# A squared-ReLU MLP by rows with a seven-product block scheme, and a small tile of its own for attention's lowest scores

## The chip, the core and the metric

The kernel runs on one core of one Trainium2 chip. The core has five engines that run side by side, each through its own instructions in order: TensorE (PE, matrix products into PSUM; PEld is its loading of the stationary operand), VectorE (DVE), ScalarE (ACT), GpSimd (POOL) and SyncE (SP, which here issues most of the DMAs). They wait for each other by semaphores. The metric is the device time of one execution in microseconds (us).

## The reference

One layer of a bidirectional encoder on 2048 tokens of 1024 features, all in float32:

```
y = rmsnorm(h) @ w_in                    # q, k, v and two convolution inputs
h = h + [dilated attention || conformer convolution] @ w_out
h = h + cross_attention(rmsnorm(h), rmsnorm(mem))
u = rmsnorm(h) @ w_up                    # 1024 -> 4096
h = h + square(relu(u)) @ w_down         # 4096 -> 1024
out = rmsnorm(h)                         # final gain norm_final_g
```

The attention has three patterns (window and dilation 128/1, 512/4, 2048/16) for each of eight heads; their outputs are weighted by a softmax over the three log-denominators. The change touches the last two lines for a quarter of the tokens, and one step of the second attention pattern.

## The kernel before

**Products in float32.** `mm3` (L198 to L201) makes each float32 product of three matmuls: each operand is split into a part that TensorE's float32r form holds and a remainder (`h` and `l`), and high x high, high x low and low x high are summed in PSUM. A weight tile is loaded by DMA (`raw`), its high part is made by a cast on ACT (L190, `whi`) and its remainder by a subtraction on DVE (L191, `wlo`); `wpost` does the three steps. Pairs of `whi` and `wlo` lie in two pools (`wp`, `wq`) with two buffers each, and `turn_w` deals them out by turns, so four pairs go round. There are two buffers for `raw`.

**Tokens.** They go in four groups of 512 (`p` = 0 to 3). `post(p)` does for one group the output projection, cross attention, the MLP and the final norm. While `post(p)` runs, the attention and the convolution of group p+1 are woven in; the last group, p = 3, has nothing woven in.

**MLP before.** Activations lie with features on the partitions and tokens along the row: the residual `hs[m]` is eight tiles of 128 features x 512 tokens. The 4096 hidden features go in eight feature groups (`fg`). Each makes four up products of 128 hidden features (24 matmuls of 128 x 128 by 128 x 512 each); DVE takes the ReLU times the row scale (L1321, `rl`), ACT squares it (L1322) and makes the high part (L1323), DVE the remainder (L1324). Then `down` makes eight products, with the weights stationary and the hidden tokens moving, 12 matmuls each, and DVE adds each PSUM result to `hs[m]` (L1339). So a feature group is 96 + 96 matmuls. In the last feature group, `add_sq` sums the squares for the final norm.

**The end before.** In the last token group the last feature group's down product is done in two halves of 256 tokens, and `final` follows each half: the root of the mean square (`rstd_from`: a matmul with ones, then DVE, a power on POOL at L177, and three small DVE operations), the gain (L1360), transposes to rows on TensorE (L1367, four to a PSUM bank), scaling by the root (L1369 on ACT, L1371 on DVE), and the DMA to the output.

**Second pattern of the attention.** `unit` works on two blocks of queries of one head. `att_probs` (L773) adds the mask to the scores and writes the lowest (scores carry the opposite sign) beside the outputs, into column HD+1 of a tile `os_` (`o1` for the second pattern), from which the DMA to `oscr` stores the pair of heads. The group p = 0 (`far`) does the third pattern with it.

**Order.** The lists of instructions are not in the code's order. The framework traces the program and a planner (`schedule_with_timeline_sim=True`) places each engine's instructions; `weave` and `pinned` only bound it. A tile's buffer is used again when its last readers are done.

Of the kernel before, what the change touches and what calls it, by code (L numbers as in the profile page):

```python
# [10 lines left out]
F32 = mybir.dt.float32  # L11
# [36 lines left out]
def hybrid_layer(ctx, tc, A, out):  # L48
# [148 lines left out]

    def mm3(o, lh, ll, rh, rl, first, end):  # L198
        PE.matmul(o, lh, rh, start=first, stop=False)  # L199
        PE.matmul(o, lh, rl, start=False, stop=False)  # L200
        last["pe"] = PE.matmul(o, ll, rh, start=False, stop=end)  # L201

# [752 lines left out]
    def att_units(p, far, then):  # L955
# [4 lines left out]
        vt = {}  # L960
        o1 = [None]
        order = (1, 0) if far else (0, 1)
# [256 lines left out]
    def post(p):  # L1219
# [87 lines left out]
        FG = 8  # L1307
        end = p == NG - 1
        for fg in range(FG):
# [16 lines left out]
            if fg == FG - 1:  # L1326
                fsum = ssum_tile(f"f{p}")
                if not end:
                    load_cat(p + 1, 0)

            def down(mp2, t, w, wh, wl):
                sl = slice(t, t + w)
                for e in range(2):
                    m = 2 * mp2 + e
                    es = slice(P * e, P * e + P)
                    pt = ps("mm", "dn")[:, 0:w]
                    for k in range(4):
                        mm3(pt, wh[:, k, es], wl[:, k, es], hh["h", k][:, sl], hh["l", k][:, sl], k == 0, k == 3)
                    last["dve"] = DVE.tensor_tensor(hs[m][:, sl], hs[m][:, sl], pt, op=ALU.add)  # L1339
                    if fg == FG - 1:  # L1340
                        add_sq(hs[m][:, sl], fsum[:, sl], m == 0)

            wd = []
            for mp2 in range(4):
                wd.append(wpost(wcols(w_down, mp2 * 256, 256, (4 * fg, 4 * fg + 4)), f"d{p}{fg}_{mp2}", (P, 4, 256)))
                if fg == FG - 1 and end:
                    continue
                down(mp2, 0, 512, *wd[-1])
                yield


        fin = {}

        def final(t, w):
            r = rstd_from(fsum[:, t:t + w])
            sl = slice(t, t + w)
            for k in range(KC):
                if t == 0:
                    fin[k] = ytile("h", k, f"fin{p}_{k}", F32)
                DVE.tensor_scalar(fin[k][:, sl], hs[k][:, sl], gain("final", k), None, op0=ALU.mult)  # L1360
            for j in range(w // P):
                c0 = t + P * j
                for g in range(2):
                    ot = ytile("l", 2 * (c0 // P) + g, f"ot{p}{c0}{g}", F32)
                    pt = ps("T", "ot")
                    for i in range(4):
                        PE.transpose(pt[:, P * i:P * i + P], fin[4 * g + i][:, c0:c0 + P], ident)  # L1367
                    if g:
                        ACT.activation(ot, pt, AF.Copy, scale=r[:, j:j + 1])  # L1369
                    else:  # L1370
                        DVE.tensor_scalar(ot, pt, r[:, j:j + 1], None, op0=ALU.mult)  # L1371
                    dma(out[0, 512 * p + c0:512 * p + c0 + P, 512 * g:512 * (g + 1)], ot)
                yield

        if end:
            for t in range(0, 512, 256):
                for mp2 in range(4):
                    down(mp2, t, 256, *wd[mp2])
                yield from final(t, 256)
        else:  # L1380
            load_cat(p + 1, 1)
            yield from final(0, 512)

# [74 lines left out]
```

## Time and profile before

| what | us |
|---|---|
| median of 3 runs (lowest to highest) | 2891.43 (2891.17 to 2894.11) |
| the profiled execution, its own time | 2888.26 |
| its span, first to last instruction | 2886.5 |
| granted TensorE clock, mean | 0.994 of full speed |
| first up matmul of the last group's MLP | at 2520.93 |
| first matmul of its last down product | at 2850.69 |
| its last matmul of a down product | at 2876.05 |

A row of a timeline reads: start, duration, engine, line, operation, written tile, read tiles, shape, count, and in brackets how long the engine had been idle before and what ended that. The recorded duration of a matmul, 0.39 us, contains its way through the array, which overlaps the next one's; the time that a matmul costs is read from start to start. A row of groups has the line, the shape and the count, then the busy time and the mean duration in ns, then the idle time before and its releasers. The windows give each engine's busy time and its instructions in a stretch of the span.

### The profile page before, as it was taken

What the parts mean: (1) busy time and instruction counts of PE and PEld (TensorE: products, weight loads), DVE (VectorE), ACT (ScalarE), POOL (GpSimd) and SP (SyncE); (2) the same over time, 40 slices, a digit from 0 to 9 for tenths busy, and PEclk for the clock granted to TensorE, in tenths of its full rate; (3) what the DMA queues carried; (4) which work ended last, traced back from release to release, by engine and by line L of the source; (5) the groups of instructions that cost most, each with busy time, mean ns of one, the idle gap of its engine ahead of it and who ended that gap; (6) DMA issues with size and microseconds to landing.
All of it is one profiled execution on the core that took longest, in us unless ns stands there. A gap on an engine that the chain in (4) does not pass through costs nothing.

```text
span 2886.5 us, 41313 instructions
## 1 busy us (share of the span) xinstructions
PE 2826.6 (98%) x15628; PEld 2376.2 (82%) x15628; DVE 1857.6 (64%) x3306; ACT 1166.3 (40%) x1988; POOL 458.0 (16%) x469
## 2 busy tenths in 40 slices
PE   8999999998999999999999999999999999999999
PEld 7878899887788888888888888888888888888887
DVE  5636535565789776557887765689876555544445
ACT  5633211475554333434543343444333433432233
POOL 1336421122102011200012012002011200000000
PEclk9999999999999999999999999999999999999999
DMA  8979845799734444554444446534543445333332
GB/s 264 295 173 228 202 132 131 182 256 247 205 102 131 135 133 123 168 160 145 121 130 130 138 117 192 175 96 128 142 127 109 139 132 175 93 90 101 96 95 74
DMA packets 598632, 433.74 MB, mean 150 GB/s; under 512 B 191550, under 2 KB 524786, under 8 KB 597921
## 3 DMA queue, kind: packets, MB, share of 16 engines
q1 hardware_dynamic: 558256, 408.21, 50.2%
q10 hardware_dynamic: 37952, 16.88, 2.4%
q0 software_dynamic: 2224, 6.01, 0.6%
q8 instruction: 123, 2.02, 0.3%
q14 instruction: 77, 0.62, 0.1%
HBM read 339.89 MB, written 91.11 MB: 149 GB/s over the span
## 4 chain that ended last, share of the span: by engine, by line
PE 82%; DVE 9%; DMA 5%; issue 2%; ACT 2%; POOL 1%; SPq 1%; POOLq 0%; DVEq 0%; ACTq 0%
PE dn L199 8%; PE dn L200 8%; PE dn L201 8%; PE up L199 7%; PE up L200 7%; PE up L201 7%; PE lin L199 4%; PE lin L201 4%; PE lin L200 4%; DVE cacc L216 3%; PE o L199 2%; PE o L200 2%; PE o L201 2%; PE xs L199 2%; PE xs L201 2%; PE xs L200 2%
## 5 line engine op out<-in xcount | busy, mean ns | idle before, releaser
L199 PE MATMUL dn<-hhh,whi_d 128*128 128x512 f32 (+1 forms) x1056 | 402.8, 392 | 7.2 <-DVE h L1339 6.1
L200 PE MATMUL dn<-hhl,whi_d 128*128 128x512 f32 (+1 forms) x1056 | 403.4, 385 | 1.1 <-DVE hhl L1324 1.1
L199 PE MATMUL up<-mh,whi_u 128*128 128x512 f32 x1024 | 402.9, 393 | 0.5 <-DVE rl L1321 0.5
L201 PE MATMUL dn<-hhh,wlo_d 128*128 128x512 f32 (+1 forms) x1056 | 402.6, 384 | 0.0
L200 PE MATMUL up<-ml,whi_u 128*128 128x512 f32 x1024 | 399.4, 390 | 1.0 <-DVE ml L1214 0.9
L201 PE MATMUL up<-mh,wlo_u 128*128 128x512 f32 x1024 | 399.7, 391 | 0.0
L216 DVE SCALAR_TENSOR_TENSOR cacc<-cu,cw,cacc 128x512 f32<-128x512 f32 x480 | 389.0, 811 | 5.5
L190 ACT CAST whi_d<-raw_d 128x1024 fp32r<-128x1024 f32 x128 | 134.6, 1052 | 418.1 <-PE up L200 378.6
L1339 DVE TENSOR_TENSOR h<-h,dn 128x512 f32<-128x512 f32 (+1 forms) x264 | 172.3, 667 | 162.9 <-PE dn L201 161.7
L190 ACT CAST whi_u<-raw_u 128x1024 fp32r<-128x1024 f32 x128 | 134.4, 1050 | 327.2 <-PE dn L200 304.1
L1321 DVE SCALAR_TENSOR_TENSOR rl<-up,ssumx 128x512 f32<-128x512 f32 x128 | 88.0, 690 | 256.9 <-PE up L201 252.6
L199 PEld LDWEIGHTS dn<-hhh,whi_d 128*128 128x128 f32 x1056 | 198.1, 189 | 47.5 <-DVE h L1339 10.2
L201 PEld LDWEIGHTS dn<-hhh,wlo_d 128*128 128x128 f32 x1056 | 198.8, 188 | 39.7
L200 PEld LDWEIGHTS dn<-hhl,whi_d 128*128 128x128 f32 x1056 | 199.3, 189 | 37.4 <-DVE hhl L1324 2.0
L200 PEld LDWEIGHTS up<-ml,whi_u 128*128 128x128 f32 x1024 | 192.4, 188 | 40.1 <-DVE ml L1214 2.3
L201 PEld LDWEIGHTS up<-mh,wlo_u 128*128 128x128 f32 x1024 | 192.2, 188 | 40.3
L199 PEld LDWEIGHTS up<-mh,whi_u 128*128 128x128 f32 x1024 | 192.4, 188 | 38.5 <-DVE rl L1321 0.9
L774 ACT ACTIVATE sm<-sm,o 128x256 f32<-128x256 f32 (+1 forms) x384 | 160.1, 466 | 126.3 <-DVE o L773 125.9
L773 DVE CUSTOM_DVE_ANT_0 sm<-s,mask 128x256 f32<-128x256 f32 (+1 forms) x384 | 128.5, 375 | 83.5 <-PE s L999 39.4
L191 DVE TENSOR_TENSOR wlo_u<-raw_u,whi_u 128x1024 fp32r<-128x1024 f32 x128 | 158.4, 1237 | 32.7 <-ACT whi_u L190 32.4
L191 DVE TENSOR_TENSOR wlo_d<-raw_d,whi_d 128x1024 fp32r<-128x1024 f32 x128 | 163.2, 1275 | 23.8 <-ACT whi_d L190 23.7
L177 POOL TENSOR_TENSOR nr<-st_v,mhalf 128x4 f32<-128x4 f32 (+1 forms) x13 | 13.0, 997 | 839.2 <-DVE st_v L173 839.2
(403 smaller groups left out, 6320.9 us busy)
## 6 DMA issues: line engine op xcount, KB each, us to landing
raw_u<-in_w_up_dram SPq DMA_DIRECT2D x128, 512.0 KB
raw_d<-in_w_down_dram SPq DMA_DIRECT2D x128, 512.0 KB
raw_o<-in_w_out_dram SPq DMA_DIRECT2D x32, 512.0 KB
raw_a<-ascr SPq DMA_DIRECT2D x32, 512.0 KB
raw_b<-bscr SPq DMA_DIRECT2D x32, 512.0 KB
k<-kscr SPq DMA_DIRECT2D x24, 512.0 KB
k<-kscr SPq DMA_DIRECT2D x8, 1152.0 KB
xn<-in_x_dram SPq DMA_DIRECT2D x32, 256.0 KB
```

The source lines that it names most:

```text
L177: POOL.tensor_tensor(dst, v, mhalf.to_broadcast([P, v.shape[1]]), op=ALU.pow)
L190: ACT.copy(hi, raw)
L191: (lo_eng or DVE).tensor_tensor(lo, raw, f(hi), op=ALU.subtract)
L199: PE.matmul(o, lh, rh, start=first, stop=False)
L200: PE.matmul(o, lh, rl, start=False, stop=False)
L201: last["pe"] = PE.matmul(o, ll, rh, start=False, stop=end)
L216: DVE.scalar_tensor_tensor(acc, u[:, t:t + 512], cw[:, c, t:t + 1], acc, op0=ALU.mult, op1=ALU.add)
L773: last["dve"] = DVE.tensor_tensor_reduce(dst, so, mask[:, 256 * m:256 * m + nk], 1.0, 3e38, ALU.add, ALU.min, mn)
L774: last["act"] = ACT.activation(dst, dst, AF.Exp, bias=mn, scale=-1.0)
L1321: last["dve"] = DVE.scalar_tensor_tensor(r, pt, 0.0, rsb, op0=ALU.max, op1=ALU.mult)
L1339: last["dve"] = DVE.tensor_tensor(hs[m][:, sl], hs[m][:, sl], pt, op=ALU.add)
```

## The change

1. *The last token group's MLP becomes `last_mlp`.* In feature group 0 the residual is transposed to rows, 128 tokens x 1024 features in four row tiles (`to_rows`, eight sets of four transposes, between up matmuls). The up products stay. The down product is now made by rows: the hidden tokens are stationary (128 at a time) and the weights move, 512 columns at a time.
2. *Seven block products for eight*, in feature groups 0 to 6. The hidden part is cut in 2 x 2 blocks of 256 tokens x 256 hidden features, the weights in 2 x 2 blocks of 256 x 512. Winograd's form of Strassen's scheme has seven block products of sums and differences of these blocks. `parts` makes the four sums of the hidden blocks on DVE and splits seven blocks in high and remainder (ACT and DVE); `sums` and one line in `seven` make four sums of weight blocks on DVE, in place in tiles that the attention had used (`room`); `piece` splits each of the seven. A product's PSUM bank is added to the row tiles by DVE, also where the next product goes on summing in the same bank (`skip_group_check`): 14 additions per feature group in place of 8.
3. *The last feature group* has plain products by rows, one row tile after the other; squares are summed along the row by ACT, and each row tile is scaled by root and gain on DVE and stored. No transposes follow, and no half products.
4. *The lowest scores of the second pattern*, in groups 1 to 3, go to a tile `low1` with two buffers, and POOL copies them beside the outputs before the store.
5. The padding tile at the head of the pool `top` shrinks from 296 to 256 columns, by what the new small tiles take, so that the tiles behind keep their addresses.

Up products, the splitting, the first seven stages and the code of groups 0 to 2 are otherwise the same; the code of `down` and `final` for them only loses its halves.

```diff
-    top.tile([P, 296], F32, name="tpad")
+    top.tile([P, 256], F32, name="tpad")
...
+                if not far:
+                    low1[0] = top.tile([P, 4, 2], F32, tag="low1", name=f"low1_{p}{pr}", bufs=2)
             os_ = o1[0] if pat else o0
+            lows = low1[0] if pat and not far else os_[:, :, :, HD + 1]
...
-                              os_[:, blk, hh, HD + 1:HD + 2]))
+                              lows[:, blk, hh:hh + 1]))
...
             if g and hh and pat:
+                if not far:
+                    POOL.tensor_copy(os_[:, :, :, HD + 1], lows)
                 dma(oscr[pr][512 * p:512 * (p + 1)].rearrange("(p b) e -> p b e", b=4),
...
+        def to_rows(g):
+            t, c = divmod(g, 2)
+            pt = ps("tr", f"hT{g}")
+            for i in range(4):
+                PE.transpose(pt[:, P * i:P * i + P], hs[4 * c + i][:, P * t:P * t + P], ident)
+            ACT.copy(row(t)[:, 512 * c:512 * c + 512], pt)
...
+        def parts(rs_, c):
+            r, j = rs_[c], c % 2
+            lo, hi = r[:, 0:256], r[:, 256:512]
+            if c < 2:
+                split([x[:, j] for x in A1], lo)
+                DVE.tensor_tensor(lo, lo, hi, op=ALU.subtract)
+                split([x[:, j] for x in S3], lo)
+            else:
+                r0 = rs_[j]
+                split([x[:, j] for x in A2], r)
+                DVE.tensor_tensor(r0[:, 256:512], r0[:, 256:512], hi, op=ALU.add)
+                DVE.tensor_tensor(r0[:, 0:256], hi, r0[:, 0:256], op=ALU.subtract)
+                split([x[j] for x in S12], r0)
+                DVE.tensor_tensor(lo, lo, r0[:, 0:256], op=ALU.subtract)
+                split([x[:, j] for x in S4], lo)
...
+        def sums(b):
+            for o, x, y_ in ((b[0, 0], b[0, 1], b[0, 0]), (b[4], b[1, 1], b[0, 0]), (b[0, 1], b[1, 1], b[0, 1])):
+                DVE.tensor_tensor(o, x, y_, op=ALU.subtract)
+
+        def seven(fg, b, first):
...
+            X, Y, Z = ([ps(kind, "dn") for _ in range(2)] for kind in ("ux", "uy", "uy"))
+            for n, (key, w, pts, more, t0, c0) in enumerate((
+                    ("A11", b[0, 0], X, False, 0, 0), ("A12", b[1, 0], Y, False, 0, 0),
+                    ("S2", b[4], X, True, 0, 1), ("S1", b[0, 0], Z, False, 2, 1),
+                    ("S3", b[0, 1], X, True, 2, 1), ("S4", b[1, 1], Z, True, 0, 1),
+                    ("A22", b[1, 0], X, True, 2, 0))):
+                wh, wl = piece(w, f"d{p}{fg}_{n}") if n else first
+                if n == 1:
+                    DVE.tensor_tensor(b[1, 0], b[1, 0], b[4], op=ALU.subtract)
+                for t in range(2):
+                    for j in range(2):
+                        mm3(pts[t], at[key](0, j, t), at[key](1, j, t), wh[:, j], wl[:, j], not more and j == 0, j == 1,
+                            more)
+                    a = row(t0 + t)[:, 512 * c0:512 * c0 + 512]
+                    last["dve"] = DVE.tensor_tensor(a, a, pts[t], op=ALU.add)
+
+        rs_ = []
+        for fg in range(FG - 1):
+            b = {4: room(4, "b")}
+            for c in range(4):
+                if c or not fg:
+                    rs_.append(hidden(fg, c))
+                for h in range(2) if 0 < c < 3 else ():
+                    b[c - 1, h] = quarter(fg, c - 1, h)
+                if c == 3:
+                    first = piece(b[0, 0], f"d{p}{fg}_0")
+                    sums(b)
+                parts(rs_, c)
+            rs_ = [hidden(fg + 1, 0)]
+            seven(fg, b, first)
...
+        for t in range(4):
+            for c in range(2):
+                pt = ps("tr", "dn")
+                for k in range(4):
+                    wh, wl = ws[c][k // 2]
+                    mm3(pt, *(x[:, k, P * t:P * t + P] for x in hh), wh[:, k % 2], wl[:, k % 2], k == 0, k == 3)
+                a = row(t)[:, 512 * c:512 * c + 512]
+                DVE.tensor_tensor(a, a, pt, op=ALU.add)
+                ACT.activation(tmp("sq"), a, AF.Square, accum_out=ss[:, 2 * t + c:2 * t + c + 1])
...
+            rstd_col(r[:, 0:1], sq, 1, top)
+            for c in range(2):
+                a = row(t)[:, 512 * c:512 * c + 512]
+                DVE.scalar_tensor_tensor(a, a, r[:, 0:1], grow[c], op0=ALU.mult, op1=ALU.mult)
+                dma(out[0, 512 * p + P * t:512 * p + P * (t + 1), 512 * c:512 * c + 512], a, nc.scalar if c else None)
```

`hidden` is the up product with ReLU and square, `quarter` the DMA of one weight block (512 KB) into a `room` tile, `split` a cast on ACT and a subtraction on DVE. The tiles of the blocks exist once, not once per feature group by turns; the four blocks of weights too.

More of the change, by code (lines that the diff above doesn't have):

```diff
@@ L196, in wcols, with mm3 @@
         return v[:, :, c0:c0 + n] if rows is None else v[:, rows[0]:rows[1], c0:c0 + n]
[L198 to L201, printed above, removed]
+    def mm3(o, lh, ll, rh, rl, first, end, more=False):
+        PE.matmul(o, lh, rh, start=first, stop=False, skip_group_check=more)
+        PE.matmul(o, lh, rl, start=False, stop=False, skip_group_check=more)
+        last["pe"] = PE.matmul(o, ll, rh, start=False, stop=end, skip_group_check=more)
     w_in, w_out = A["w_in"][0], A["w_out"][0]
@@ L960, in att_units @@
         vt = {}
-        o1 = [None]
+        o1, low1 = [None], [None]
         order = (1, 0) if far else (0, 1)
@@ L1307, in post @@
         FG = 8
-        end = p == NG - 1
+        if p == NG - 1:
+            last_mlp(hs, y, rsb)
+            return
         for fg in range(FG):
@@ L1327, in post, with down @@
                 fsum = ssum_tile(f"f{p}")
[L1328 to L1332, printed above, removed]
+                load_cat(p + 1, 0)
+            def down(mp2, wh, wl):
                 for e in range(2):
@@ L1340, in down @@
                     if fg == FG - 1:
-                        add_sq(hs[m][:, sl], fsum[:, sl], m == 0)
-            wd = []
+                        add_sq(hs[m], fsum, m == 0)
             for mp2 in range(4):
[L1345 to L1348, printed above, removed]
+                down(mp2, *wpost(wcols(w_down, mp2 * 256, 256, (4 * fg, 4 * fg + 4)), f"d{p}{fg}_{mp2}", (P, 4, 256)))
@@ L1349, in post @@
                 yield
+        load_cat(p + 1, 1)
+        r = rstd_from(fsum)
         fin = {}
-        def final(t, w):
-            r = rstd_from(fsum[:, t:t + w])
-            sl = slice(t, t + w)
-            for k in range(KC):
[L1358 to L1382, printed above, removed]
+        for k in range(KC):
+            fin[k] = ytile("h", k, f"fin{p}_{k}", F32)
+            DVE.tensor_scalar(fin[k], hs[k], gain("final", k), None, op0=ALU.mult)
+        for j in range(4):
+            c0 = P * j
+            for g in range(2):
+                ot = ytile("l", 2 * j + g, f"ot{p}{c0}{g}", F32)
+                pt = ps("T", "ot")
+                for i in range(4):
+                    PE.transpose(pt[:, P * i:P * i + P], fin[4 * g + i][:, c0:c0 + P], ident)
+                if g:
+                    ACT.activation(ot, pt, AF.Copy, scale=r[:, j:j + 1])
+                else:
+                    DVE.tensor_scalar(ot, pt, r[:, j:j + 1], None, op0=ALU.mult)
+                dma(out[0, 512 * p + c0:512 * p + c0 + P, 512 * g:512 * (g + 1)], ot)
+            yield
```

71 lines of the change are left out of this document (68 added, 3 removed).

## The prediction

> **What bounds the kernel now.** I read the head of the page first, then its chain of work that ended last.
>
> ```profile
> span 2886.5 us, 41313 instructions
> PE 2826.6 (98%) x15628; PEld 2376.2 (82%) x15628; DVE 1857.6 (64%) x3306; ACT 1166.3 (40%) x1988; POOL 458.0 (16%) x469
> PE 82%; DVE 9%; DMA 5%; issue 2%; ACT 2%; POOL 1%; SPq 1%; POOLq 0%; DVEq 0%; ACTq 0%
> ```
>
> TensorE works in 98% of the span and carries 82% of the chain, so a matmul taken away is worth its whole slot, if whatever feeds TensorE keeps up. The page has only averages; the stage that is changed is the last group's MLP, so next the busy times by stretch. From 2567.81 on, each stretch is one eighth of that MLP (192 matmuls), then come the last four up products, the last down product, and what follows the last matmul.
>
> ```profile
> core 0: us, PE busy (x) PEld busy (x) DVE busy (x) ACT busy (x) POOL busy (x), PEclk, DMA share, GB/s
> 2567.81:2611.33 43.52, 43.52 (x193) 35.83 (x192) 20.36 (x24) 12.86 (x17) 0.00 (x0) 1.00 0.33 97
> ...
> 2828.93:2850.69 21.76, 21.76 (x97) 18.02 (x96) 9.62 (x11) 7.68 (x11) 0.00 (x0) 1.00 0.24 73
> 2850.69:2876.33 25.64, 25.60 (x215) 25.39 (x214) 20.37 (x52) 9.65 (x20) 0.70 (x1) 1.00 0.09 33
> 2876.33:2886.50 10.17, 3.21 (x21) 2.25 (x18) 3.35 (x9) 1.79 (x3) 0.70 (x1) 0.75 0.33 126
> ```
>
> TensorE has no gap here: 43.52 us in 43.52. VectorE is busy for 20.4 of them, ScalarE for 12.9, DMA a third. Only behind the last matmul, 10.17 us, does TensorE stand.
>
> **Term 1, seven products for eight.** One unit of 24 matmuls, from its first to the next unit's first, and the same where the moving operand is weights and the stationary one tokens, as the new down product has it:
>
> ```profile
> 2828.93 0.39 PE L199 MATMUL up<-mh,whi_u 128*128 128x512 f32 x1
> 2834.37 0.39 PE L199 MATMUL up<-mh,whi_u 128*128 128x512 f32 x1
> ...
> 2442.31 0.39 PE L199 MATMUL xs<-whi_a,yh 128*128 128x512 f32 x1
> 2447.75 0.39 PE L199 MATMUL xs<-whi_a,yh 128*128 128x512 f32 x1
> ```
>
> Both take 5.44 us, 0.2267 each, so swapping the operands costs nothing. A block product is 2 token tiles x 2 hidden tiles x 3 = 12 matmuls, 2.72 us. Seven of the eight feature groups lose one: 7 x 2.72 = **-19.0 us**. A feature group then lasts 43.52 - 2.72 = 40.8 us on TensorE.
>
> **Term 2, what VectorE must do in 40.8 us.** Its groups in six such stretches of before, and three pairs of neighbours that show how closely it starts one behind another:
>
> ```profile
> L1339 DVE TENSOR_TENSOR h<-h,dn 128x512 f32<-128x512 f32 x47 | 31.2, 686 | 61.7 <-PE dn L201 61.7
> L191 DVE TENSOR_TENSOR wlo_d<-raw_d,whi_d 128x1024 fp32r<-128x1024 f32 x24 | 29.4, 1226 | 4.0 <-ACT whi_d L190 4.0
> L1324 DVE TENSOR_TENSOR hhl<-rl,hhh 128x512 fp32r<-128x512 f32 x24 | 16.6, 693 | 0.0
> L1321 DVE SCALAR_TENSOR_TENSOR rl<-up,ssumx 128x512 f32<-128x512 f32 x24 | 16.6, 692 | 68.8 <-PE up L201 68.8
> ...
> 1956.68 1.22 DVE L191 TENSOR_TENSOR wlo_b<-raw_b,whi_b 128x1024 fp32r<-128x1024 f32 x1
> 1957.81 0.68 DVE L1212 TENSOR_TENSOR h<-x,h 128x512 f32<-128x512 f32 x1
> ...
> 2179.37 1.27 DVE L1339 TENSOR_TENSOR h<-h,dn 128x512 f32<-128x512 f32 x2
> ...
> 2856.93 0.42 DVE L1339 TENSOR_TENSOR h<-h,dn 128x256 f32<-128x256 f32 x1
> 2857.27 0.42 DVE L1165 TENSOR_TENSOR ssumf<-ssumf,sq 128x256 f32<-128x256 f32 x1
> ```
>
> Per feature group the new code gives VectorE 4 `rl` (0.69), 4 + 7 = 11 weight remainders (1.23), 4 weight sums of 1024 (not in before; priced as the remainder of the same shape, 1.23), 14 additions into the sums (0.69, before 8), and in `parts` 2 x 3 operations of 256 (0.42) and 2 x (2 of 512 + 4 of 256). Full durations: 2.8 + 13.5 + 4.9 + 9.7 + 2.5 + 6.1 = **39.5 us**. But neighbours overlap: the 1.22 one is followed after 1.13, two of 0.68 take 1.27 together, 0.42 is followed after 0.34. Some 51 operations by 0.08 is 4.1, so by starts it is **35.4 us**, 87% of 40.8. ScalarE needs 11 casts (1.05), 4 squares and some ten copies, about 19 us, and is no bound.
>
> [...]
>
> What a VectorE so full does to TensorE, before shows in another stage:
>
> ```profile
> 1948.00:2021.00 73.00, 72.43 (x409) 59.50 (x409) 68.19 (x115) 35.32 (x59) 17.34 (x16) 1.00 0.46 128
> ```
>
> VectorE 93% busy, and TensorE loses 0.57 us of 73. That is 0.3 us in 40.8, **+2.2 us** over seven groups. Bounds: nothing, and the rivals below. The cover is a lead in time. The planner, not the code, orders the engines:
>
> ```profile
> 2824.55 1.23 DVE L191 TENSOR_TENSOR wlo_u<-raw_u,whi_u 128x1024 fp32r<-128x1024 f32 x1 [0.17 <-ACT whi_u L190]
> 2826.41 0.69 DVE L1339 TENSOR_TENSOR h<-h,dn 128x512 f32<-128x512 f32 x1 [0.64 <-PE dn L201]
> ...
> 2828.90 1.05 ACT L190 CAST whi_u<-raw_u 128x1024 fp32r<-128x1024 f32 x1 [4.39 <-PE dn L200]
> ```
>
> The remainder of a later up weight is made at 2824.55, ahead of an addition that the code writes before it. The cast at 2828.90 is the last of an up weight, used from 2834.37 + 2 x 5.44 = 2845.25: four pairs of weight tiles in rotation give 16 us. With products of 2.72 us this shrinks to about two products, 5.4 us, less 1.05 + 1.23 + 0.2 = 3 us to spare; a PSUM bank is written again 4.1 us after it can be read (one product and one token tile). A VectorE that runs 3 to 4 us behind stops TensorE, one that is 1.5 us behind does not. The DMAs move: as many bytes, in 2 KB rows, the `quarter` loads queue on SP behind the previous group's splits and ahead of the next up weights; these splits are done in the middle of the previous products, and DMA is busy a third of the time. Zero; if a load came late, one up weight behind it would have 5 us of lead to lose.
>
> **Term 3, transposes go to the start.** `to_rows` puts 8 x 4 transposes between up matmuls. A set of four between two matmuls in before:
>
> ```profile
> 2454.54 0.39 PE L201 MATMUL xs<-whi_a,yl 128*128 128x512 f32 x1
> 2454.77 0.60 PE L1264 MATMUL ptx<-ident,xp 128*128 128x128 f32 x4
> 2455.12 0.48 PE L199 MATMUL xs<-whi_a,yh 128*128 128x512 f32 x1
> ```
>
> 0.58 - 0.23 = 0.35 us each, **+2.8 us**. The ones that `final` did fall into the next term.
>
> **Term 4, the last down product and the end.**
>
> ```profile
> 2876.05 0.28 PE L201 MATMUL dn<-hhh,wlo_d 128*128 128x256 f32 x1
> 2876.37 0.42 DVE L1339 TENSOR_TENSOR h<-h,dn 128x256 f32<-128x256 f32 x1
> 2876.89 0.42 ACT L1164 ACTIVATE sq<-h 128x256 f32<-128x256 f32 x1 [1.02 <-DVE h L1339]
> 2878.46 0.16 DVE L173 TENSOR_SCALAR st_v<-nps 128x2 f32<-128x2 f32 x1 [0.70 <-PE nps L1174]
> 2880.01 0.75 DVE L1371 TENSOR_SCALAR ot<-ot,nr 128x512 f32<-128x512 f32 x1
> 2882.36 0.75 DVE L1371 TENSOR_SCALAR ot<-ot,nr 128x512 f32<-128x512 f32 x1 [1.59 <-PE ot L1367]
> ...
> L1253 ACT ACTIVATION_READ_ACCUMULATOR xp<-xs,xmx,nr 128x1 f32 x16 | 3.3, 207 | 0.0
> ```
>
> Before, 2850.69 to 2886.50 is 35.8 us. After: 96 matmuls x 0.2267 = 21.8; 0.2 to the addition; 0.69; square of 512 with sum 0.1 + 0.62 + 0.21; add 0.2; scale 0.2; the power on POOL and three small ones, 2878.46 to 2880.01 less the first, 1.35; two scalings by gain and root, 0.75 + 0.66; from the last scaling's end to the end of the span as in before, 2886.50 - 2883.11 = 3.4. Sum 30.2, **-5.6 us**. Its risk: the fourth hidden tile's split comes 3 us behind its up product, and the last of four weight pairs waits for that product too. Before covers the same by taking other sums first (0.04 us of idle in its 25.64); the four banks of `tr` allow it again. I take +0.3, bounds 0 and 2.
>
> **Term 5, the lowest scores.** Their old tile waits for the store of the pair before:
>
> ```profile
> DVE sm L773 <- DMA oscr<-o: 11.1, 4, 5.0
> ...
> 1627.10 0.42 DVE L773 CUSTOM_DVE_ANT_0 sm<-s,mask 128x256 f32<-128x256 f32 x1 [4.96 <-DMA oscr<-o]
> 1630.77 0.50 PE L199 MATMUL dn<-hhh,whi_d 128*128 128x512 f32 x1 [1.30 <-DVE h L1339]
> ...
> L925 POOL TENSOR_TENSOR csm<-csm 128x8 f32<-128x8 f32 x8 | 2.9, 368 | 0.6
> ```
>
> The longest of the four reached TensorE, by 1.3 us: **-1.3 us**; bounds 0 (the wait moves to the next user of the old tile) and -11.1 (all of it). The new POOL copy (12, about 0.37 us each) is waited for by the store on ACT's queue, and ACT's casts stand behind that; POOL's longest neighbour is under 3 us, and a weight cast has more lead than that. Zero.
>
> **Sum**: -19.0 + 2.2 + 2.8 - 5.6 + 0.3 - 1.3 = **-20.6 us**. The profiled execution took 2888.3, so it would take 2867.7; the runs' median, 2891.4, is 3.2 above it, and I apply the difference to that: **2871**.
>
> **Rivals.** [...]
> (b) *Slower: the turn from up to products.* The code writes the weight sums and the last `parts` behind the fourth up product. If the planner leaves them there, VectorE has from that product's end until the third block product 5.44 + 2 x 2.72 = 10.9 us for: two `rl` 1.4, three sums 3.7, the `parts` of two hidden tiles 6.1, two additions 1.4, four remainders 4.9, in all 17.5. TensorE stands 6.6 us in each of seven groups, 46 in place of 2.2: 2915. It decides from 14.2 us on (3.3 of standing, 23 in all, cancels the gain). For it: single tiles for the split parts and sums leave no second group to work ahead in. Against it: the loads for the sums land during the products before, and the row at 2824.55 shows work pulled forward.
> (c) *The gain is eaten, no change*: the same turn with the sums done early, 13.8 us of work, 2.9 of standing, 20 in all: 2889.
> (d) *The new tile does not do what it says*: the values of the second pattern still go into the old tile and may wait for its store in turn; worth the 1.3 us of term 5, inside the range.
>
> **How the numbers follow.** Forecast 0.60 (2863 to 2876), rival (a) 0.22 (2876 to 2885.6), (c) 0.07, (b) 0.11. The lower end is the sum without terms of waiting and with another third of what term 5 could bring, 2891.4 - 23.1 - 4 = 2864. The upper end closes behind rival (a), 2886, and leaves out (b), (c) and the little below. About 0.2%, 5.8 us, is what a measurement of this kernel can tell from no change: faster 0.82, same 0.07, slower 0.11.
>
> **What would show it.** In the profile after: 84 matmuls fewer in the down groups and 0.2267 from start to start; feature groups of 40.8 to 41.2 us; VectorE 36 to 38 us busy in each; no TensorE wait on `dn` above 0.5 us; about 8.3 us from the last matmul to the end; no wait of L773 on `oscr` from the second group on. [...] A TensorE wait of several us, once per group, on a split or a weight sum before the second or third block product would be (b) or (c), and proves the lead in term 2 wrong.

## The result and the profile after

| | before | after |
|---|---|---|
| median (lowest to highest), 4 runs each, us | 2892.77 (2891.17 to 2895.64) | 2860.68 (2857.01 to 2865.75) |
| ratio, 95% interval | | 0.9889 (0.9871 to 0.9907) |
| the profiled execution, its span, us | 2888.26, 2886.5 | 2865.75, 2864.0 |
| first up matmul of p = 0 | 892.61 | 898.79 |
| first up matmul of p = 3 | 2520.93 | 2520.58 |
| first matmul of the last down product | 2850.69 | 2833.74 |

The kernel became faster by 1.1%, more than forecast: 2860.7 lies below the range of 2864 to 2886. The head of the page after, in the same three lines:

```profile
span 2864.0 us, 41201 instructions
PE 2807.4 (98%) x15440; PEld 2359.9 (82%) x15440; DVE 1960.8 (68%) x3473; ACT 1206.4 (42%) x2055; POOL 467.7 (16%) x483
PE 83%; DVE 8%; DMA 5%; issue 1%; ACT 1%; POOL 1%; SPq 1%; DVEq 0%; POOLq 0%; ACTq 0%
```

The averages hardly move, so the table's marks cut the execution into stretches. From the first up matmul of p = 3 to the end of the span ("the last MLP" below) before took 365.6 us and after takes 343.4: **-22.2**. From the first up matmul of p = 0 to that of p = 3 ("the middle") before took 1628.3 and after 1621.8: **-6.5**, where the only edit is the tile for the lowest scores. The first 890 us went the other way by 6.2; there both traces run TensorE's 5508 matmuls in the same order, and the experiments show that this stretch varies between executions of one kernel.

The last MLP by windows (column order as in the prediction: length, then PE, PEld, DVE, ACT and POOL busy with counts, granted clock, DMA share, GB/s). A group here reaches from one group's second up product to the next one's, so that the planner's choices shift a product in or out of it (43.5 us hold 192 matmuls of 0.2267, 40.8 us hold 180); then the last down product, and what follows the last matmul:

```profile
2564.18:2607.99 43.81, 43.81 (x195) 36.26 (x195) 40.19 (x59) 20.20 (x27) 0.00 (x0) 1.00 0.41 122
...
2692.30:2733.11 40.81, 40.81 (x182) 33.80 (x181) 36.17 (x52) 18.52 (x25) 0.00 (x0) 1.00 0.35 104
2733.11:2773.91 40.80, 40.80 (x182) 33.80 (x181) 36.16 (x52) 18.52 (x25) 0.00 (x0) 1.00 0.34 104
...
2833.74:2855.55 21.81, 21.81 (x97) 17.84 (x95) 13.51 (x31) 7.16 (x17) 1.67 (x3) 1.00 0.13 49
2855.55:2863.97 8.42, 0.12 (x1) 0.00 (x0) 2.93 (x9) 0.72 (x2) 0.55 (x1) 0.76 0.33 127
```

A steady group is 40.8 us with TensorE busy in all of it, although VectorE is busy for 36.2 of them, 89%. Even the second group, in which VectorE works 40.19 of 43.81 us (92%), has no gap. The list of waits of this stretch has one row for TensorE (total, times, longest):

```profile
PE dn L200 <- ACT hqh L1397: 0.5, 1, 0.5
```

Why the turn from up to products costs nothing, the timeline of VectorE shows. The group's second, third and fourth up products run from 2651.51 to 2667.8:

```profile
2657.55 1.23 DVE L191 TENSOR_TENSOR wlo_d<-b,whi_d 128x1024 fp32r<-128x1024 f32 x1 [0.40 <-ACT whi_d L190]
2658.81 1.22 DVE L1464 TENSOR_TENSOR b<-b,b 128x1024 f32<-128x1024 f32 x1
2659.96 0.68 DVE L1409 SCALAR_TENSOR_TENSOR rl<-up,ssumx 128x512 f32<-128x512 f32 x1
2660.56 1.22 DVE L1464 TENSOR_TENSOR mask<-b,b 128x1024 f32<-128x1024 f32 x1
2661.69 1.22 DVE L1464 TENSOR_TENSOR b<-b,b 128x1024 f32<-128x1024 f32 x1
```

L1464 are the three weight sums (`mask` is a tile of the attention that holds one of them). The code has them behind the fourth up product; the planner put them at 2658.8 to 2662.9, while the third runs, with the first weight remainder ahead of them.

In the middle, the waits of L773 (L774 after) on `oscr` and on `dn` are gone; only those for scores, which `sm` always had, are left (`sm` is the masked scores; rows of the whole trace):

```profile
DVE sm L774 <- PE s L1003: 45.2, 36, 4.9
...
DVE sm L774 <- PE s L858: 23.0, 22, 3.8
```

### The profile page after: what moved, and what is told of

It is laid out like the page before. It is cut to its first block, busy times and chain, and to the rows that moved or that the text cites. A ratio compares the mean times of both kernels' runs of the same rounds, so it can differ in the third digit from the quotient of the medians.

```text
span 2864.0 us, 41201 instructions
## 1 busy us (share of the span) xinstructions
PE 2807.4 (98%) x15440; PEld 2359.9 (82%) x15440; DVE 1960.8 (68%) x3473; ACT 1206.4 (42%) x2055; POOL 467.7 (16%) x483
## 4 chain that ended last, share of the span: by engine, by line
PE 83%; DVE 8%; DMA 5%; issue 1%; ACT 1%; POOL 1%; SPq 1%; DVEq 0%; POOLq 0%; ACTq 0%
PE dn L200 8%; PE dn L201 8%; PE dn L202 8%; PE up L200 7%; PE up L202 7%; PE up L201 7%; PE lin L200 4%; PE lin L202 4%; PE lin L201 4%; PE o L200 2%; PE o L202 2%; PE o L201 2%; DVE cacc L217 2%; PE xs L200 2%; PE xs L202 2%; PE xs L201 2%
## 5 line engine op out<-in xcount | busy, mean ns | idle before, releaser
L200 PE MATMUL dn<-hhh,whi_d 128*128 128x512 f32 x768 | 299.1, 399 | 1.1 <-ACT hhh L1331 1.1
L201 PE MATMUL dn<-hhl,whi_d 128*128 128x512 f32 x768 | 298.7, 391 | 0.7 <-DVE hhl L1332 0.7
L202 PE MATMUL dn<-hhh,wlo_d 128*128 128x512 f32 x768 | 298.2, 391 | 0.0
L190 ACT CAST whi_d<-raw_d 128x1024 fp32r<-128x1024 f32 x100 | 105.1, 1051 | 319.9 <-PE up L201 281.5
L1345 DVE TENSOR_TENSOR h<-h,dn 128x512 f32<-128x512 f32 x192 | 128.6, 683 | 84.7 <-PE dn L202 83.9
L774 DVE CUSTOM_DVE_ANT_0 sm<-s,mask 128x256 f32<-128x256 f32 (+1 forms) x384 | 128.6, 375 | 69.0 <-PE s L1003 45.2
L202 PEld LDWEIGHTS dn<-hhh,wlo_d 128*128 128x128 f32 x768 | 144.2, 188 | 30.7
L200 PEld LDWEIGHTS dn<-hhh,whi_d 128*128 128x128 f32 x768 | 143.7, 188 | 29.7 <-ACT hhh L1331 1.3
L201 PEld LDWEIGHTS dn<-hhl,whi_d 128*128 128x128 f32 x768 | 144.6, 188 | 28.3 <-DVE hhl L1332 1.5
L775 ACT ACTIVATE sm<-sm,o 128x256 f32<-128x256 f32 (+1 forms) x288 | 116.5, 454 | 55.7 <-DVE o L774 55.3
L191 DVE TENSOR_TENSOR wlo_d<-raw_d,whi_d 128x1024 fp32r<-128x1024 f32 x100 | 128.2, 1282 | 14.2 <-ACT whi_d L190 14.1
```

The lines of the kernel that those rows point to most:

```text
L190: ACT.copy(hi, raw)
L191: (lo_eng or DVE).tensor_tensor(lo, raw, f(hi), op=ALU.subtract)
L200: PE.matmul(o, lh, rh, start=first, stop=False, skip_group_check=more)
L201: PE.matmul(o, lh, rl, start=False, stop=False, skip_group_check=more)
L202: last["pe"] = PE.matmul(o, ll, rh, start=False, stop=end, skip_group_check=more)
L774: last["dve"] = DVE.tensor_tensor_reduce(dst, so, mask[:, 256 * m:256 * m + nk], 1.0, 3e38, ALU.add, ALU.min, mn)
```

## The experiments

"MLP" and "middle" are the two stretches defined above, in us, from the first up matmuls and the end of each profiled execution. Ratios are to before, run beside them: its medians were 2892.77 beside after, 2890.88 beside e1 to e4, 2888.42 beside e5 to e8 and 2888.07 beside e9 to e11.

| run | median | ratio (95%) | first up, p = 0 | middle | MLP |
|---|---|---|---|---|---|
| before, the profile shown | | | 892.6 | 1628.3 | 365.6 |
| after, the profile shown | 2860.68 | 0.9889 (0.9871 to 0.9907) | 898.8 | 1621.8 | 343.4 |
| e1_both | 2854.55 | 0.9873 (0.9858 to 0.9888) | 885.4 | 1619.4 | 343.5 |
| e2_low_only | 2877.04 | 0.9951 (0.9938 to 0.9965) | 887.0 | 1621.0 | 365.7 |
| e3_mlp_only | 2864.99 | 0.9912 (0.9898 to 0.9927) | 890.8 | 1626.8 | 343.5 |
| e4_rows_eight | 2872.14 | 0.9938 (0.9925 to 0.9952) | 894.6 | 1619.3 | 361.5 |
| e5_null | 2886.81 | 1.0001 (0.9991 to 1.0011) | 887.0 | 1626.5 | 365.8 |
| e6_pad_only | 2887.97 | 1.0000 (0.9991 to 1.0009) | 892.2 | 1631.7 | 365.8 |
| e7_dve_half | 2867.10 | 0.9931 (0.9913 to 0.9949) | 892.9 | 1620.5 | 355.6 |
| e8_dve_full | 2879.29 | 0.9961 (0.9948 to 0.9974) | 892.0 | 1620.3 | 365.8 |
| e9_sums_late | 2864.09 | 0.9919 (0.9896 to 0.9942) | 888.1 | 1619.8 | 357.1 |
| e10_seven_all | 2857.42 | 0.9899 (0.9884 to 0.9915) | 888.0 | 1620.6 | 343.8 |
| e11_dve_quarter | 2859.68 | 0.9904 (0.9881 to 0.9926) | 886.3 | 1619.8 | 349.4 |

### Which part brought the time

e1_both is the kernel after once more. e2_low_only is before with the new tile alone:

```diff
+                if not far:
+                    low1[0] = top.tile([P, 4, 2], F32, tag="low1", name=f"low1_{p}{pr}", bufs=2)
...
+            lows = low1[0] if pat and not far else os_[:, :, :, HD + 1]
...
-                              os_[:, blk, hh, HD + 1:HD + 2]))
+                              lows[:, blk, hh:hh + 1]))
...
+                if not far:
+                    POOL.tensor_copy(os_[:, :, :, HD + 1], lows)
```

e3_mlp_only is after without it:

```diff
-                if not far:
-                    low1[0] = top.tile([P, 4, 2], F32, tag="low1", name=f"low1_{p}{pr}", bufs=2)
...
-            lows = low1[0] if pat and not far else os_[:, :, :, HD + 1]
+            lows = os_[:, :, :, HD + 1]
...
-                if not far:
-                    POOL.tensor_copy(os_[:, :, :, HD + 1], lows)
```

Both also resize the padding tile by what the small tiles take or leave.

> The changed kernel again, on the chip that runs its parts. By the stages of the two profiles the change is worth 22.2 us in the last MLP and 6.5 us between the first and the last MLP, 28.7 in all; the first 730 us hold the same instructions in both and differ by 6.4 us in the profiled executions by chance. Theory A (stages only): 28 to 30 us faster than before. Theory B (the medians' 32 us hold something that the two profiles do not show, in the first 730 us): 32 us or more again.

> Only the lowest scores of the second pattern in a tile of their own; the last MLP as before. Theory A (three waits of about 5 us on the store, two of which the profile puts down to a matmul that has nothing to do with the scores, each cost TensorE 1.3 to 2.4 us): 6 to 7 us faster than before, and no TensorE wait of the down product on the addition L1345 in any group. The prediction's term (only the wait whose row names the store counts): 1.3 us faster, and two waits of 2.4 us stay. Rival (the wait moves to the copy of the values): no change.

> The last MLP changed, the lowest scores as before. Theory A: 22 us faster than before, in the profile the last MLP from its first up matmul to the end 343 to 344 us against 365.6 us, and the three waits of 2.4, 1.3 and 2.4 us back. Rival (the gain between the MLPs comes from another order of the planner, not from the tile): 28 us faster, waits gone here too.

The two parts add up by stages and do not touch one another: the MLP is 343.4 to 343.5 with `last_mlp` and 365.6 to 365.8 without, whichever tile is used. The middle separates as cleanly: 1626.5 to 1631.7 in four profiles with the old tile (before, e3, e5, e6; mean 1628.35), 1619.3 to 1621.8 in nine with the new one (mean 1620.27). So the tile is worth **8.1 us** on average, not 1.3. By stages e2 and e3 thus meet their first theories; by its median e2 gained 13.8 us, more than its stages hold, and e1's 36.3, which meet its theory B, are more than its stages too (see what stays open).

e4_rows_eight keeps rows, the new end and the new tile, but makes eight plain products by rows in every feature group:

```diff
...
-                parts(rs_, c)
-            rs_ = [hidden(fg + 1, 0)]
-            seven(fg, b, first)
...
+                split([x[c] for x in hh], hidden(fg, c))
+            for c in range(2):
...
+                for t in range(4):
+                    pt = ps("tr", "dn")
+                    for k in range(4):
+                        wh, wl = w2[k // 2]
+                        mm3(pt, *(x[k][:, P * t:P * t + P] for x in hh), wh[:, k % 2], wl[:, k % 2], k == 0, k == 3)
```

> The last MLP by rows, with eight plain block products in every feature group (96 matmuls, no sums of blocks, 8 additions); the rest as changed. Theory A (the seven products give their 84 matmuls whole, 19.0 us): 19 us slower than the changed kernel, so about 10 us faster than before, and from the first matmul of the last down product to the end 30.3 us as in the changed kernel. Rival (VectorE's doubled work costs TensorE time that the profile hides): under 15 us slower than the changed kernel.

One of its groups, and all from its last down product (first matmul at 2845.88) on:

```profile
2650.04:2693.56 43.52, 43.52 (x194) 36.06 (x192) 20.13 (x25) 13.05 (x16) 0.00 (x0) 1.00 0.32 97
2845.88:2875.35 29.47, 21.92 (x97) 17.85 (x95) 16.42 (x39) 7.88 (x19) 2.21 (x4) 0.96 0.19 71
```

The groups are before's 43.5 again. From the first up matmul to the last down product it takes 332.0 us, before 329.8, after 313.2. So the transposes to rows cost 2.3, and the seven products save 18.9 of the 19.0 that 84 matmuls at 0.2267 make: the expectation's theory A. The end is 29.5 here and 30.2 after, in place of 35.8.

### Is the middle's gain a matter of addresses, or of being another kernel?

e5_null is before as a kernel of its own; e6_pad_only allots the new tile's room at the same place and leaves it unused:

```diff
-    top.tile([P, 296], F32, name="tpad")
+    top.tile([P, 280], F32, name="tpad")
...
+                if not far:
+                    top.tile([P, 4, 2], F32, tag="low1", name=f"low1_{p}{pr}", bufs=2)
```

> The kernel before, submitted as a kernel of its own: the same instructions. Theory A (the stretch up to the first up matmul takes 885 to 899 us in profiled executions of the same instructions, by chance of the load): within 7 us of before, and what its own median differs is the size of error that an interval over rounds does not contain. Theory C (the first stretch depends on the kernel): 0, within 2 us.

> The kernel before with the padding tile at the head of the pool top made 16 columns smaller and 16 columns of unused tiles taken where the new tiles for the lowest scores are: small tiles lie at other addresses, nothing else changes. Theory A: like before, and from the first up matmul to the end 1993 to 1995 us as in the profile of before. Theory C (the addresses of the small tiles give the 6 us that the tile alone has more in its median, 13.8, than in its stages, 7.2): 6 us faster than before.

Both are at 1.000 of before, with middles among those of the old tile, so neither addresses nor being another kernel made the 8.1 us. e5's 1.6 us fit both of its theories. e6 took 1997.5 us from the first up matmul to the end, more than its theory A allowed; the waits below account for it. The table also shows how much the first 890 us vary: 885.4 to 898.8 among profiles of kernels whose code is the same there, and 13 us between two executions of one kernel (after and e1). Nothing of the gain is to be read from it.

What e6 adds is a key to the waits. In before, two rows besides the `oscr` row of the prediction (whose 11.1 us are 4 waits):

```profile
DVE sm L773 <- PE dn L201: 10.4, 2, 5.2
...
PE dn L199 <- DVE h L1339: 6.1, 3, 2.4
```

In e6, where L773 does exactly the same work:

```profile
DVE sm L773 <- DMA oscr<-o: 16.7, 5, 5.6
DVE sm L773 <- PE dn L200: 5.4, 1, 5.4
...
PE dn L199 <- DVE h L1341: 7.8, 3, 2.7
```

Six waits, some 22 us, both times; but of three long ones, some 5 us each, one bears the name `oscr` in before and two in e6. The waits of the stretch from 1060 to 1100 alone, in before and in e6:

```profile
DVE sm L773 <- PE dn L201: 5.2, 1, 5.2
```

```profile
DVE sm L773 <- DMA oscr<-o: 5.6, 1, 5.6
```

It is the same wait at the same place under two names, and masking scores needs nothing from a down product. In e5, which has before's instructions one for one, this wait bears the store's name too (5.1 us); in all, e5 has 15.4 us in 5 waits under `oscr` and 5.2 in 1 under `PE dn`. All three are the wait for the store; in before, two were put down to another engine's last event. Each held up VectorE, and TensorE behind it: three waits on `h`, not one. In e2 and after these rows are gone; in e3 `PE dn <- DVE h` is back with 6.3 us in 3 times.

The waits are not all. The first of the three in before, on VectorE and then on TensorE:

```profile
1077.92 0.42 DVE L773 CUSTOM_DVE_ANT_0 sm<-s,mask 128x256 f32<-128x256 f32 x1 [5.21 <-PE dn L201]
...
1078.61 3.19 DVE L216 SCALAR_TENSOR_TENSOR cacc<-cu,cw,cacc 128x512 f32<-128x512 f32 x3
1081.73 0.68 DVE L1339 TENSOR_TENSOR h<-h,dn 128x512 f32<-128x512 f32 x1
...
1082.46 0.77 PE L199 MATMUL dn<-hhh,whi_d 128*128 128x512 f32 x1 [2.42 <-DVE h L1339]
1083.03 0.63 PE L200 MATMUL dn<-hhl,whi_d 128*128 128x512 f32 x1
1083.46 0.63 PE L201 MATMUL dn<-hhh,wlo_d 128*128 128x512 f32 x1
...
1085.98 0.40 PE L201 MATMUL dn<-hhh,wlo_d 128*128 128x512 f32 x1
1086.22 0.40 PE L199 MATMUL dn<-hhh,whi_d 128*128 128x512 f32 x1
```

`sm` waits 5.2 us, the convolution stands ahead of the addition on VectorE, and the bank of `dn` is free 2.4 us late. Then the matmuls start 0.43 us apart instead of 0.2267: the nine steps from 1082.46 to 1086.22 take 3.76 us instead of 2.04, another 1.7 us. The granted clock is the third number from the end of a window's row; here the 3.41 us up to the end of this wait and the 3.42 us behind it, and the same for the third wait, which is as long (2.41 us, up to 2178.84):

```profile
1079.10:1082.51 3.41, 0.99 (x18) 0.79 (x15) 3.34 (x5) 1.61 (x3) 1.09 (x1) 1.00 0.42 113
1082.51:1085.93 3.42, 3.42 (x8) 2.73 (x9) 3.42 (x5) 0.00 (x0) 0.00 (x0) 0.50 0.00 0
2174.78:2178.19 3.41, 1.65 (x21) 1.32 (x19) 3.34 (x6) 2.31 (x4) 1.08 (x1) 1.00 0.51 132
2178.19:2181.61 3.42, 2.77 (x12) 2.31 (x13) 3.42 (x5) 0.00 (x0) 0.00 (x0) 1.00 0.00 0
```

The clock was halved for 3.41 us behind the first wait and not behind the third. The rows are cut at 1082.51, where the half clock begins, and at whole multiples of 3.4133 us from there; the last section tells why. The first wait lies whole within one row, in which TensorE is busy for 0.99 of 3.41 us. The third is cut at 2178.19: in the row ahead of the cut TensorE is busy for 1.65 us, and the clock stays at 1.00.

So 6.1 us of waits, 1.7 at half clock, and 0.1 of a slow first step behind each of the other two (0.33 us from 1630.77 and 0.34 from 2178.84, instead of 0.2267): 8.0 us, against 8.1 measured. That these agree to 0.1 is luck. In the other three profiles with the old tile, waits on `h` and half clock make 6.3 + 1.7 = 8.0 us (e3), 5.1 + 1.7 = 6.8 (e5) and 7.8 + 5.1 = 12.9 (e6, half clock in three stretches behind two of its waits), and their middles lie 6.5, 6.3 and 11.5 above the new tile's mean. So the sum follows the measured time from profile to profile, to some 1.5 us.

### How near is VectorE to being the bound?

Three kernels give VectorE one or two extra additions to a spare tile behind each of the 49 block products (one of 512 in e7, two in e8, one of 256 in e11):

```diff
+                DVE.tensor_tensor(junk, rsb, rsb, op=ALU.add)
...
+        junk = zp.tile([P, 512], F32, tag="z6", name="junk6")
```

> One VectorE addition of 128x512 more behind each block product (seven per feature group, 0.6 us each from start to start, 4.2 in all; its result is not used): VectorE goes from 36.2 to 40.4 us busy of 40.8. By starts it still fits: feature groups 40.8 to 41.8 us, the last MLP 343 to 350 us. By full durations (39.5 + 4.8 = 44.3 us of work) the group would last 44.3 us or more, the last MLP 368 us.

> Two such additions behind each block product, in all 14 per feature group: 36.2 + 8.4 = 44.6 us of VectorE work by starts, above 40.8. By starts VectorE is the bound: feature groups of 44.6 to 46 us, the last MLP 370 to 380 us. By full durations (39.5 + 9.6 = 49.1): 49 us, 401 us. If the cover is something else than VectorE's time, it stays below 350.

> The new kernel with one extra VectorE addition of 128x256 in each of the 49 block products, written to a spare tile: 7 x 0.34 = 2.4 us a group, so VectorE is busy for 36.2 + 2.4 = 38.6 of 40.8 us, 94.6%. One addition of 128x512 a product (4.8 us, 100%) cost 12 us in all, none cost nothing. If VectorE is covered up to about 95%, the last MLP stays at 343 to 345 us. If the cost is in proportion to the added work from the first on, it is 349 to 350. The new kernel's own margin to the bound is above 2.4 us a group in the first case and below it in the second.

e7 and e8 met none of their expectations: 355.6 and 365.8. e11 gave 349.4, the value for a cost in proportion; but not for that reason. All three expectations supposed that the additions spread over the groups as written. The groups of operations say otherwise (shortest, median and longest in ns, then first and last start), for e7 and for e11:

```profile
L1487 DVE TENSOR_TENSOR junk<-ssumx x49: 677/684/689, 2532.9 to 2674.3; 128x512 f32<-128x512 f32 x49
```

```profile
L1487 DVE TENSOR_TENSOR junk<-ssumx x49: 409/417/425, 2525.6 to 2636.7; 128x256 f32<-128x256 f32 x49
```

They depend on nothing, so the planner put them all ahead, in three to four groups, until VectorE was full. The windows of e11, whose extra work ends at 2636.7:

```profile
2554.00:2597.52 43.52, 42.55 (x187) 34.57 (x185) 42.41 (x72) 18.75 (x26) 0.00 (x0) 1.00 0.34 99
2597.52:2640.17 42.65, 41.84 (x181) 33.47 (x180) 40.52 (x68) 18.33 (x25) 0.00 (x0) 1.00 0.32 98
2640.17:2680.97 40.80, 40.80 (x181) 33.78 (x180) 37.02 (x54) 18.84 (x25) 0.00 (x0) 1.00 0.37 114
```

So these runs are read by stretches. The last two rows hold 180 matmuls each, in 42.65 us and in 40.80: TensorE loses 1.9 us in the middle row, with VectorE busy for 95%. The first row loses 1.5, at 97% (186 matmuls in 43.52 us). Idle time shows only 0.8 and 1.0 of that: a matmul may start late by the 0.16 us that two recorded durations overlap (0.39 less 0.2267) before an idle time appears. The other 2.5 us of e11's 6.0 lie in its first group, where VectorE works without a break from 2535.0 on. At 91% (37.02 of 40.80) nothing is lost.

A bound by VectorE's share does not come out of this, because a group of e7 loses nothing at 99% (39.15 of 39.44), all its 174 matmuls being 0.2267 apart, and e9 below loses 1.1 us a group at 86%:

```profile
2655.06:2694.50 39.44, 39.44 (x176) 32.66 (x174) 39.15 (x59) 17.39 (x24) 0.00 (x0) 1.00 0.34 97
```

In e7 and e8 the long waits of TensorE, up to 1.9 us, are for the addition that empties a PSUM bank (`rowsh`, L1486). So what costs is an addition that comes late, and how much more work the new kernel could carry if it were spread over the groups was not measured.

In e8 VectorE is full until the end. One of its groups, the first and the last of the 18 rows of what VectorE does in it (busy time, mean ns), and the window:

```profile
L1488 DVE TENSOR_TENSOR junk<-ssumx 128x512 f32<-128x512 f32 x13 | 8.9, 684 | 0.0
...
L1427 DVE TENSOR_TENSOR rl<-rl 128x256 f32<-128x256 f32 x1 | 0.4, 418 | 0.0
```

```profile
2783.24:2826.05 42.81, 41.58 (x182) 33.56 (x181) 42.63 (x63) 17.71 (x23) 0.00 (x0) 1.00 0.21 61
```

The 18 rows sum to 47.6 us of recorded durations, done in 42.8 us: by starts VectorE got through 11% more here than its durations say. The 98 additions, 0.6 us each by starts, are 59 us; the room in seven groups is 7 x 4.6 = 32; the 27 left over are near the 22.4 measured. This count is no rule: for e7 it leaves nothing over (29 us against 32), and e7 lost 12.2, of which 3.4 are two stretches at half clock.

### What the planner's lead is worth

e9_sums_late binds the three weight sums to their place in the code:

```diff
-                    sums(b)
+                    with ExitStack() as st:
+                        after(st, "dve")
+                        sums(b)
```

> The new kernel with its three weight sums bound, on VectorE's list, to stand behind the ReLU product of the fourth up product, where the code writes them; the new kernel's planner had put them among the first up products. Nothing else is changed. If that lead is what keeps rival (b) away, TensorE now stands at every turn from up to products: rivals (b) and (c) give 2.9 to 6.6 us in each of seven groups, so the last MLP takes 363 to 390 us instead of 343.4, and the list of waits shows some seven waits of TensorE of 2 us or more. If the work left behind the fourth up product is less than rival (b) counted (the sums alone move there, 3.7 us), it is under 1.3 us a group, and the last MLP takes 343 to 352 us.

It came out between the two, at 357.1. Its first stretch and a steady group, and then TensorE's waits in the last MLP:

```profile
2507.87:2563.31 55.44, 49.84 (x232) 40.16 (x230) 34.90 (x55) 25.40 (x39) 1.01 (x1) 0.97 0.16 50
...
2603.83:2645.70 41.87, 41.64 (x181) 33.55 (x180) 35.83 (x52) 18.53 (x25) 0.00 (x0) 1.00 0.33 101
```

```profile
PE dn L200 <- DVE rowsh L1486: 4.7, 7, 3.5
PE dn L200 <- ACT rl L1410: 2.1, 1, 2.1
```

A steady group is 41.87, 1.1 us longer, with VectorE no busier than before. The first group, which has no earlier products to work behind, stands 2.1 and 3.5 us and then runs eight matmuls at half clock. Compared matmul by matmul with after, it loses 7.5 us of the 13.7, and each of the six others some 1.0. So the price of a missing lead, as rival (b) has it, is real where nothing can go ahead; elsewhere the rest of the work (remainders, `parts`) still has its lead, and only the sums' 3.7 us are late.

### A version with seven products everywhere

```diff
-        for fg in range(FG - 1):
+        for fg in range(FG):
...
-            rs_ = [hidden(fg + 1, 0)]
+            rs_ = [hidden(fg + 1, 0)] if fg < FG - 1 else []
...
-                pt = ps("tr", "dn")
-                for k in range(4):
-                    wh, wl = ws[c][k // 2]
-                    mm3(pt, *(x[:, k, P * t:P * t + P] for x in hh), wh[:, k % 2], wl[:, k % 2], k == 0, k == 3)
...
-                DVE.tensor_tensor(a, a, pt, op=ALU.add)
```

> The new kernel with seven products in all eight feature groups; the plain last group is gone, and all rows are ended behind its last product. TensorE loses 12 more matmuls, 2.7 us. Against it: in the last group no up product of a next group covers the turn from up to products (0 to 4 us), and the last two row tiles get their last additions together, so that the end behind the last matmul grows by some 1.5 us. Last MLP 343.4 - 2.7 + 1.5 + 0 to 4, so 342 to 346 us. If all of that is covered, 341, and the kernel beats both; if it is 344 or more, plain products in the last group are the better choice.

The MLP takes 343.8, the kernel after 343.4: no gain. The last 12 matmuls are gone (2.7 us) and TensorE does not wait, but the end behind the last matmul, 8.4 us in after, is longer here:

```profile
2841.00:2852.40 11.40, 0.00 (x0) 0.00 (x0) 7.64 (x22) 2.04 (x8) 1.40 (x3) 0.72 0.48 185
```

That is 3.0 us, twice what was expected: in the plain last group three of the four row tiles are ended beside TensorE's work, in this one two tiles get their last sums together. None of these kernels is faster than after by its stages.

## Why the prediction was right and wrong

**The step that failed is term 5.** The prediction put it: "The longest of the four reached TensorE, by 1.3 us: -1.3 us", and of its lower bound, all of the 11.1 us, it let 5.3 into the range (the 1.3 and another 4). Two things were missed. It counted the waits that bear the store's name; the two of 5.2 us put down to `PE dn` are the store's as well (e6, e2), and the row `PE dn <- DVE h`, 6.1 us in 3 times, was the sum to take. And it took a wait of TensorE at its own length; one of the three was followed by 1.7 us at half clock. 8.1 us measured in place of 1.3 takes the forecast from 2871 to 2864, the lower edge of the range; term 2, which cost nothing, takes it below.

**Term 2** was mis-sized: +2.2 forecast, nothing measured. The demand was right (35.4 us forecast by starts, 36.2 busy), but its price was carried over from a stage at 93% by the share of busy time, and the share does not set the price: 99% cost nothing in a group of e7, 86% cost 1.1 us in e9. What covers is the lead that the prediction named beside it, and in the new groups it suffices. The chance of 0.22 for rival (a), VectorE as the bound, and the range's upper end of 2886 rest on the 39.5 us of full durations as the demand; no run shows such a demand: a group of e8 did 47.6 us of durations in 42.8 us, and the new groups take 40.8.

**Term 1** held: 18.9 of 19.0 (e4 against after). **Term 3**: 2.3 of 2.8. **Term 4**: the last down product and the end take 30.2 us, forecast 30.2 + 0.3; behind the last matmul 8.4, forecast 8.3. Together the MLP gave 22.2 us instead of the 19.3 of terms 1 to 4; of the difference, 2.2 are term 2, 0.5 term 3 and 0.3 term 4, less 0.1 of term 1. The zero for the new POOL copy in term 5 is neither shown nor refuted: TensorE's waits behind POOL in the middle are 0.2 to 0.9 us with the old tile and 0 to 1.5 with the new one.

**The rivals.** (a) VectorE as the bound did not come: 40.8 us a group at 89%; how much more work would bring it is open, since the added work of e7, e8 and e11 was not spread over the groups. (b) and (c) did not come because the sums are made during the third up product, as the row at 2824.55 had suggested; e9, which takes this lead from the sums alone, costs 13.7 us; (b)'s 46, with the last `parts` late too, was not run. (d) fell: no wait on `oscr` is left.

**What stays open.** MLP and middle together give 22.2 + 8.1 = 30.3 us; the medians differ by 32.1 (after) and 36.3 (e1). The rest of 2 to 6 us was not located. It is of the size by which the first 890 us vary, and the nine runs of before beside e1 lay between 2882.1 and 2895.3. But it has one sign: each of the ten runs with changed code (after, e1 to e4, e7 to e11) gained more by its median than by its two stretches, by 0.7 to 7.4 us. They share four sets of runs of before, so these are not ten separate proofs, and chance is argued here, not shown.

## What to carry to other kernels

A name behind a wait is a guess: where equal waits recur at one instruction and one name makes no sense for it, add them up, and take the price from what the bound engine waits for behind them. A stall of TensorE of about 2 us can cost nearly twice its length (2.42 us and 1.7 more at half clock in before, 1.94 and 1.6 more in e7), so small stalls in a dense stream are worth removing. And before an engine is called too full, look at how far ahead of need its work can be placed: here a group with VectorE 99% busy cost nothing (e7), while three sums bound to a late place cost 13.7 us at 86%.

## What the runs showed of the hardware that was not expected

TensorE got half its clock for 3.41 us inside a stream that was otherwise dense (before, 1082.51 to 1085.93), and the length of the wait ahead did not decide it: 2.42 us was followed by half clock and 2.41 us was not (before, both above), and 1.94 us was (e7, below). In before the half-clock stretches begin whole multiples of 3.4133 us apart: behind the one at 659.26, those at 707.05, 730.94 and 1082.51 follow after 14, 7 and 103 times that length. Cut at such multiples, the row ahead of 1082.51 has TensorE idle for 2.42 us, and the third wait falls apart into 1.76 and 0.65. That the idle time of one such row counts is the author's reading of these cases. It gives no border: in the first 890 us of before the clock fell to half behind a row with 1.47 us idle (727.53 to 730.94) and stayed full behind one with 1.74 (505.66 to 509.07). In e7 the wait of 1.94 us came behind one of 0.42 in the same row, which has 2.21 us idle:

```profile
2646.62 0.79 PE L200 MATMUL dn<-whi_d,hz 128*128 128x512 f32 x1 [1.94 <-DVE rowsh L1486]
```

```profile
2643.06:2646.47 3.41, 1.20 (x5) 0.33 (x3) 3.41 (x6) 1.45 (x2) 0.00 (x0) 1.00 0.49 159
2646.47:2649.88 3.41, 3.26 (x8) 2.58 (x9) 3.41 (x8) 0.00 (x0) 0.00 (x0) 0.50 0.43 154
```

Eight matmuls in 3.4 us instead of fifteen; TensorE counts as busy nearly all the while, so a busy share doesn't show it, and only the granted clock and the steps from start to start do.
